# A hybrid decoder layer on one core: one negated copy of the inverse's product bank, one pool of 14 head slots, memory key products in attention's bank, plain scores in four heads

## The chip, the core and the metric

The kernel runs on one core of a Trainium2 chip. A core has five engines with queues of their own: TensorE (PE: matmul, with the weight load, PEld, as a row of its own), VectorE (DVE), ScalarE (ACT), GpSimd (POOL) and SyncE (SP), which here issues the DMA transfers. Results of TensorE land in PSUM, which has eight banks of 128 partitions x 512 fp32; everything else lies in SBUF. The metric is the device time of one execution in microseconds (us), the median of several runs.

## The reference

The trunk has one layer with these inputs: 2048 tokens of width 1024. The token mixer is a gated DeltaNet with 8 heads of width 128 (chunks of 64 in the reference; the kernel uses 128) and, in parallel, cross-attention of 4 heads to 256 memory rows. Both outputs are joined and projected; then come a squared-ReLU MLP of width 4096 and two post-norms. Cut to what the change touches:

```python
lower = where(strict, einsum('bnhcd,bnhsd->bnhcs', k_beta, kc) * decay, 0.0)
a_mat = eye(CHUNK) + lower
u = triangular_solve(a_mat, v_beta, lower=True, unit_diagonal=True)
w = triangular_solve(a_mat, k_beta * exp(gc)[..., None], lower=True, unit_diagonal=True)
attn_qk = einsum('bnhcd,bnhsd->bnhcs', qc, kc) * decay
# scan over chunks, per head:
v_new = u_c - w_c @ state
o = qd @ state + a_c @ v_new
state = state * dc + kd.T @ v_new
# memory:
mem_kv = layer_norm(mem, mem_ln_g, mem_ln_b) @ w_mem_kv
p = softmax(q @ mem_k.T * 128 ** -0.5);  m = p @ mem_v
```

## The kernel before

**Tiles and stages.** The tokens are worked in four blocks of 512 (`TB`), each as four chunks of 128 (`NC`). Two blocks make a half. In a half, `mixer` runs twice (blocks 0 and 1, then 2 and 3), then `out_seven` projects the joined heads of both blocks, `ff1` and `ff2` do the MLP. The three big products are formed by a Strassen-like scheme of seven products. In the profile the first mixer pair fills 0 to about 640 us, the first output projection reaches to 788, the MLP to 1405; the second half follows from there.

**Number formats.** Most products are made of three matmuls on rounded operands (`mm3`): an fp32 value is split into a rounded part hi (a cast on ACT) and a remainder lo (a subtraction on DVE), and hi x hi, hi x lo and lo x hi are added in PSUM. The small products of the DeltaNet are plain fp32 matmuls; each shows as two matmul rows in the trace.

**A head.** `dense` projects q, k and v, applies the convolution and the activation, splits q and k into the tiles kq (hi and lo, one buffer each), and transposes k into kd. `gdn_a` loads the decay rows (gb), builds the decay matrices dl and at, forms the scores pkq of k against k and q, and calls `invert`. `invert` computes the inverse of a unit triangular matrix of 128 per chunk, all four chunks at once: columns of 16 on DVE, and then three joining steps of 16 to 32, 32 to 64 and 64 to 128, each of two products through the banks pq and pp and copies between tiles (Lq, ZP, X32, X64, YP, Y). In the middle step the bank pp is read by a DVE transpose into Lq, and by two multiplications by -1 on DVE and two on ACT into Y. Two further DVE multiplications by -1 place the transposed values into X64. `gdn_b` runs the recurrence chunk by chunk: state, R, vt, state again; at each step TensorE needs the DVE or ACT result before.

**Buffers.** Tiles of 128 x 512 for the heads come from the slot tags s0 and s1, seven each; even heads take s0, odd heads s1 (kd, gb, dl, at, Y, vb, qd). The output projection and the MLP take operand parts from the same tags: xl of the third output product (S3) and of the last (A22) from s1, xl of S4 from s0. PSUM: `acc` has three banks (projections, and the memory keys and values), `ga0` and `ga1` one each (scores, transposes and inverse of even and odd heads), `pb` two (recurrence), `m` one (memory attention).

**Memory.** In block 0, steps 1 to 4 of the head loop also do the memory: `memory_rows` normalizes and transposes it, `memory_keys` loads a weight column, splits it, and forms one head's keys (24 matmuls of 256 columns) in a bank of `acc`, which ACT and DVE then split to a staging tile; two heads per step. `memory_values` does the values. Attention to the memory (`mem_attn`) starts at step 5 of a block.

**Order.** Nothing is issued as written. `Recorder` keeps every operation with its reads and writes; `issue` then plans an order with a price for each operation (`cost`), a delay for each hand-over between engines (`LAT`, `LAT_FROM`, `MARGIN`), free slots of each tag, and a priority, which is the place in the program plus `shift`. The instructions are then emitted in the order of planned starts, and each engine works its queue strictly in that order. A `gate` holds DMA issues back until a given operation. Because all operations are recorded by one helper, the profile gives line 402 for nearly all.

Of the kernel before, what the change touches and what calls it, by code (L numbers as in the profile page):

```python
# [14 lines left out]
P = 128  # L15
# [19 lines left out]
MARGIN = 100  # L35
# [149 lines left out]
class Op:  # L185
    __slots__ = ("i", "eng", "fn", "args", "kw", "dur", "extra", "succ", "npred", "ready", "start", "end", "load", "last",
                 "bufs", "prio", "quads", "cols", "late", "lhs")


class Recorder:  # L190
# [15 lines left out]
    def add(self, eng, fn, name, args, kw):  # L206
        o = Op()
        o.i, o.eng, o.fn, o.args, o.kw = len(self.ops), eng, fn, args, kw
        o.succ, o.npred, o.ready, o.extra = [], 0, 0, 0
# [12 lines left out]
        preds = {}  # L222
# [68 lines left out]
    def issue(self):  # L291
# [50 lines left out]
        while True:  # L342
# [76 lines left out]
def hybrid_layer(  # L419
# [40 lines left out]
    BUFS = {"d": 11, "th": 2, "s0": 7, "s1": 7, "on": 1, "iv": 4}  # L460
# [334 lines left out]
    def dense(b, h, T, G, w0=None):  # L795
        res = {}
        for nm, o in (("q", QO), ("k", KO), ("v", VO)):
# [19 lines left out]
            if nm in "qk":  # L817
# [6 lines left out]
        kd = res["kd"] = slot("kd", "s%d" % (h % 2))  # L824
# [26 lines left out]
    def invert(L, par):  # L851

        Lq = small("Lq", [P, 32, NC], 2)
        for q in range(4):
            r = slice(32 * q, 32 * q + 32)
            nc.scalar.copy(out=Lq[r].rearrange("p f c -> p c f"), in_=L[r, :, 32 * q:32 * q + 32])
# [11 lines left out]
        nc.vector.tensor_scalar_mul(Lc, Lq[:, 0:16], half[:, 0:1])  # L868
        nc.vector.scalar_tensor_tensor(out=Lc, in0=Lq[:, 16:32], scalar=half[:, 1:2], in1=Lc,
# [22 lines left out]
        Y = slot("Y", "s%d" % par)  # L892
# [24 lines left out]
        ZP = Lq.rearrange("p f c -> p (f c)")[:, :64].rearrange("p (c f) -> p c f", c=2)  # L917
# [6 lines left out]
        for p in range(2):  # L924
            for u, eng in ((0, nc.gpsimd), (1, nc.vector)):
                q = quads[2 * p + u]
                eng.tensor_copy(X32[q, :, q].part((u, p)), Z[64 * p:64 * p + 32, 2 * u:2 * u + 2])
        for p in range(2):
            for u, eng in ((0, nc.gpsimd), (1, nc.vector)):
                q = quads[2 * u + p]  # L930
                eng.tensor_copy(X64[q, :, q].part((u, p)), Z[quads[p], 2 * u:2 * u + 2])
# [43 lines left out]
    def gdn_a(h, r, G):  # L975
# [4 lines left out]
        gb = slot("gb", "s%d" % par)  # L980
# [11 lines left out]
        dl = slot("dl", "s%d" % par)  # L992
# [5 lines left out]
        at = slot("at", "s%d" % par)  # L998
# [18 lines left out]
        vb = slot("vb", "s%d" % par)  # L1017
# [3 lines left out]
        qd = slot("qd", "s%d" % par)  # L1021
# [83 lines left out]
    MB = "m"  # L1105
    KEEP_FF = {2: 0, 3: 1, 4: 2}
# [152 lines left out]
    def second_half(ys, T0d, B, between):  # L1259

        homes = {"T3": [slots("d", 4), slots("s0", 4)], "T2": [slots("d", 3), slots("s0", 3), halves("kq0", 1)],
                 "T4": [slots("s1", 3), slots("th", 2), slots("on", 1), halves("kq1", 1)],
                 "T1": [halves("tok", 4)], "B22": [slots("s1", 4), slots("iv", 4)]}
# [30 lines left out]
        for k in K2:  # L1294
            t4[k] = slot("b21", "s1")
# [129 lines left out]
    def ff2(s, x1d):  # L1425
# [35 lines left out]
        def xpart(n, u, last):  # L1461
# [6 lines left out]
            for j in range(2):  # L1468
                hi, lo = slot("xh", "d", F32R), slot("xl", "s%d" % j, F32R)
# [150 lines left out]
    def out_seven(s, x1d, T0d):  # L1620
# [208 lines left out]
```

## Time and profile before

| | us |
|---|---|
| median of three runs | 2762.95 |
| lowest and highest run | 2762.62, 2763.29 |
| the profiled execution, its own time | 2760.71 |
| its span, first to last instruction | 2759.0 |
| TensorE busy in the span | 2719.8 (99%) |
| VectorE busy | 2112.2 (77%) |
| ScalarE busy | 1642.3 (60%) |
| GpSimd busy | 403.7 (15%) |

The profile is of one execution. A row of a group or of a timeline gives engine, operation, output <- inputs, partitions x elements, how often, and after it the idle time of that engine just before and what ended it. A releaser is inferred from semaphores: where the engine named had long been done, it was another. TensorE's granted clock is 1.00 at full speed; the mean over the span is 0.997.

### The profile page before, as it was taken

What the parts mean: (1) busy time and instruction counts of PE and PEld (TensorE: products, weight loads), DVE (VectorE), ACT (ScalarE), POOL (GpSimd) and SP (SyncE); (2) the same over time, 40 slices, a digit from 0 to 9 for tenths busy, and PEclk for the clock granted to TensorE, in tenths of its full rate; (3) what the DMA queues carried; (4) which work ended last, traced back from release to release, by engine and by line L of the source; (5) the groups of instructions that cost most, each with busy time, mean ns of one, the idle gap of its engine ahead of it and who ended that gap; (6) DMA issues with size and microseconds to landing.
All of it is one profiled execution on the core that took longest, in us unless ns stands there. A gap on an engine that the chain in (4) does not pass through costs nothing.

```text
span 2759.0 us, 42405 instructions
## 1 busy us (share of the span) xinstructions
PE 2719.8 (99%) x13589; PEld 2267.0 (82%) x13589; DVE 2112.2 (77%) x5652; ACT 1642.3 (60%) x4082; POOL 403.7 (15%) x1030
## 2 busy tenths in 40 slices
PE   9999999999999999999999999999999999999998
PEld 7888888887788888888888888888887788888887
DVE  7889889998777777665778887888978665657575
ACT  7678767676485556334446676677855655544342
POOL 3233223321000000000023321223201000000000
PEclk9999999999999999999999999999999999999999
DMA  8565558876788888766754344444578744477673
GB/s 327 207 234 205 215 182 288 290 258 228 269 284 302 280 285 297 268 211 205 265 209 149 138 155 174 169 147 159 206 251 280 249 145 152 163 252 243 205 239 116
DMA packets 208543, 613.99 MB, mean 223 GB/s; under 512 B 23072, under 2 KB 32192, under 8 KB 188352
## 3 DMA queue, kind: packets, MB, share of 16 engines
q1 hardware_dynamic: 207888, 611.23, 63.5%
q8 instruction: 107, 1.75, 0.2%
q14 instruction: 116, 0.95, 0.1%
q10 hardware_dynamic: 432, 0.05, 0.0%
HBM read 436.54 MB, written 174.65 MB: 222 GB/s over the span
## 4 chain that ended last, share of the span: by engine, by line
PE 88%; ACT 7%; DVE 4%; issue 1%; POOL 1%; DMA 0%; DVEq 0%; SPq 0%; POOLq 0%; ACTq 0%
PE f2A L402 13%; PE fA L402 12%; PE ao L402 8%; PE f2C L402 6%; PE fC L402 6%; PE az L402 5%; PE aq L402 5%; PE av L402 5%; PE ak L402 5%; PE f2B L402 3%; PE fB L402 3%; PE amq L402 3%; PE pc L402 3%; PE po L402 2%; PE pkq L402 1%
## 5 line engine op out<-in xcount | busy, mean ns | idle before, releaser
L402 DVE TENSOR_TENSOR whl<-wraw,whl 128x512 fp32r<-128x512 f32 (+2 forms) x294 | 257.2, 884 | 109.4 <-ACT whl L402 107.0
L402 ACT CAST whl<-wraw 128x512 fp32r<-128x512 f32 (+2 forms) x294 | 226.5, 780 | 158.0 <-PE fC L402 52.0
L402 PE MATMUL fA<-B,whl 128*128 128x512 f32 x1152 | 277.2, 389 | 1.8 <-ACT B L402 1.5
L402 ACT CAST X<-X 128x1024 fp32r<-128x1024 f32 x118 | 123.9, 1052 | 236.2 <-DMA X<-xsc 196.2
L402 PE MATMUL f2A<-whl,X 128*128 128x512 f32 x1152 | 262.1, 389 | 0.0
L402 PEld LDWEIGHTS fA<-B,whl 128*128 128x128 f32 x1152 | 216.1, 188 | 47.5 <-ACT B L402 1.9
L402 PEld LDWEIGHTS f2A<-whl,X 128*128 128x128 f32 x1152 | 216.2, 188 | 44.9
L402 DVE TENSOR_TENSOR X<-X,X 128x1024 fp32r<-128x1024 f32 x118 | 144.2, 1223 | 129.0 <-ACT X L402 128.8
L402 PE MATMUL aq<-T,whl 128*128 128x512 f32 x768 | 214.3, 408 | 10.0 <-ACT T L402 5.5
L402 PE MATMUL az<-T,whl 128*128 128x512 f32 x768 | 213.0, 406 | 0.0
L402 PE MATMUL ak<-T,whl 128*128 128x512 f32 x768 | 211.4, 406 | 0.0
L402 PE MATMUL av<-T,whl 128*128 128x512 f32 x768 | 210.4, 404 | 0.0
L402 PE MATMUL fC<-B,whl 128*128 128x512 f32 x768 | 185.4, 389 | 0.3 <-DVE B L402 0.3
L402 PE MATMUL f2C<-whl,X 128*128 128x512 f32 x768 | 174.7, 389 | 0.0
L402 PEld LDWEIGHTS fC<-B,whl 128*128 128x128 f32 x768 | 144.1, 188 | 30.7 <-DVE B L402 0.8
L402 PEld LDWEIGHTS f2C<-whl,X 128*128 128x128 f32 x768 | 144.1, 188 | 29.9
L402 PEld LDWEIGHTS aq<-T,whl 128*128 128x128 f32 x768 | 136.5, 191 | 32.7 <-ACT T L402 5.5
L402 POOL TENSOR_SCALAR ve<-mv 128x1 f32<-128x1 f32 x34 | 16.4, 483 | 962.0 <-DVE mv L402 961.5
L402 PEld LDWEIGHTS av<-T,whl 128*128 128x128 f32 x768 | 137.3, 189 | 22.7
L402 PEld LDWEIGHTS ak<-T,whl 128*128 128x128 f32 x768 | 136.4, 189 | 23.5
L402 PEld LDWEIGHTS az<-T,whl 128*128 128x128 f32 x768 | 135.9, 189 | 21.6
L402 PE MATMUL ao<-whl,X 128*128 128x512 f32 x528 | 140.1, 404 | 3.5 <-DVE whl L402 1.3
(287 smaller groups left out, 6300.8 us busy)
## 6 DMA issues: line engine op xcount, KB each, us to landing
whl<-wsc SPq DMA_DIRECT2D x108, 1024.0 KB, 4.8
wraw<-in_w_ff_dram SPq DMA_DIRECT2D x106, 512.0 KB, 4.5
X<-xsc SPq DMA_DIRECT2D x96, 512.0 KB, 3.9
wsc<-whl SPq DMA_DIRECT2D x36, 1024.0 KB, 5.2
whl<-tsc SPq DMA_DIRECT2D x64, 512.0 KB, 4.7
xsc<-hB SPq DMA_DIRECT2D x96, 256.0 KB, 3.4
xo<-cat SPq DMA_DIRECT2D x80, 256.0 KB, 3.9
wraw<-in_w_in_dram SPq DMA_DIRECT2D x35, 512.0 KB, 5.9
```

What stands on the lines that cost most here:

```text
L402: o.fn(*[res(a) for a in o.args], **{k: res(v) for k, v in o.kw.items()})
```

## The change

- **Planner.** Two reads of one PSUM bank from different engines are now ordered in the plan, with a hand-over of 40 ns (`TURN`); before, the plan let them run together.
- **Pool.** The tags s0 and s1 of seven slots become one tag s0 of 14. Every use of s1, in the heads, the output projection and the MLP, takes s0.
- **Memory keys.** The product goes to bank `m` in place of a bank of `acc`, and the load and split of its weights are planned 400 places earlier.
- **Scores.** In heads 5, 6 and 7 of block 1 and head 7 of block 3 (`PLAIN`), q and k are not split, and the scores are two plain fp32 products of 128 columns per chunk in place of three rounded ones of 256.
- **Inverse.** Lq is laid out chunk by chunk, so its four copies write contiguous rows, and Lc reads it with a stride. The four copies into X32 are all on DVE and the four into X64 all on POOL; before, each set was half and half. In the middle step ACT makes one negated copy of bank pp in SBUF (`Nf`, in the second half of Lq), and the transpose, the copies into Y (two DVE, two ACT) and the two into X64 read from it.

```diff
-MARGIN = 100
+MARGIN, TURN = 100, 40
...
+                    elif r.buf.psum and q.eng != eng and not is_w and not qw:
+                        turns[q.i] = q
...
+        for i, q in turns.items():
+            if i not in preds:
+                preds[i] = q
+                q.turns.add(o.i)
...
-                s.ready = max(s.ready, o.end + lat)
+                s.ready = max(s.ready, o.end + (TURN if s.i in o.turns else lat))
...
-    BUFS = {"d": 11, "th": 2, "s0": 7, "s1": 7, "on": 1, "iv": 4}
+    BUFS = {"d": 11, "th": 2, "s0": 14, "on": 1, "iv": 4}
...
     def memory_keys(h):
+        rec.shift = -400
         w = load_cols(w_mem_k, h)
-        a = bank("amk", "acc")
+        rec.shift = 0
+        a = bank("amk", "m")
...
-            if nm in "qk":
+            if nm in "qk" and (b, h) not in PLAIN:
...
-        Lq = small("Lq", [P, 32, NC], 2)
+        Lq = small("Lq", [P, NC, 32], 2)
...
-            nc.scalar.copy(out=Lq[r].rearrange("p f c -> p c f"), in_=L[r, :, 32 * q:32 * q + 32])
+            nc.scalar.copy(out=Lq[r], in_=L[r, :, 32 * q:32 * q + 32])
...
-            for u, eng in ((0, nc.gpsimd), (1, nc.vector)):
+            for u in range(2):
                 q = quads[2 * p + u]
-                eng.tensor_copy(X32[q, :, q].part((u, p)), Z[64 * p:64 * p + 32, 2 * u:2 * u + 2])
+                nc.vector.tensor_copy(X32[q, :, q].part((u, p)), Z[64 * p:64 * p + 32, 2 * u:2 * u + 2])
...
-                eng.tensor_copy(X64[q, :, q].part((u, p)), Z[quads[p], 2 * u:2 * u + 2])
+                nc.gpsimd.tensor_copy(X64[q, :, q].part((u, p)), Z[quads[p], 2 * u:2 * u + 2])
...
-        tr = Lq.rearrange("p f c -> p (f c)")[:64, 64:].part("t")
-        nc.vector.transpose(tr, pb[:64])
+        Nf = Lq.rearrange("p c f -> p (c f)")[:, 64:]
+        nc.scalar.activation(Nf, pb, AF.Copy, scale=-1.0)
+        tr = Lq.rearrange("p c f -> p (c f)")[:64, :64]
+        nc.vector.transpose(tr, Nf[:64])
+        N3 = Nf.rearrange("p (c f) -> p c f", c=2)
         for p in (1, 0):
             o = Y3[64 * p:64 * p + 32, :, 64 * p + 32:64 * p + 64]
-            nc.vector.tensor_scalar_mul(o[:, 2:4], pp[quads[2 * p + 1]], -1.0)
-            nc.scalar.activation(o[:, 0:2], pp[quads[2 * p]], AF.Copy, scale=-1.0)
+            nc.vector.tensor_copy(o[:, 2:4], N3[quads[2 * p + 1]])
+            nc.scalar.copy(out=o[:, 0:2], in_=N3[quads[2 * p]])
...
-            nc.vector.tensor_scalar_mul(X64[quads[2 * u + 1], :, quads[2 * u]].part((u, 2)), tr[quads[u]].part("t"), -1.0)
+            nc.vector.tensor_copy(X64[quads[2 * u + 1], :, quads[2 * u]].part((u, 2)), tr[quads[u]])
...
-        kh, kl = r["kq"]
+        kh, kl = r.get("kq", (None, None))
...
-                mm3(pkq[:, c - c0], kh[:, 0, cs], kl[:, 0, cs], kh[:, :, cs], kl[:, :, cs], True, True)
+                if kh is None:
+                    for u, x in enumerate((k, q)):
+                        nc.tensor.matmul(pkq[:, c - c0, u], k[:, cs], x[:, cs], start=True, stop=True)
+                else:
+                    mm3(pkq[:, c - c0], kh[:, 0, cs], kl[:, 0, cs], kh[:, :, cs], kl[:, :, cs], True, True)
...
+    PLAIN = {(1, 5), (1, 6), (1, 7), (3, 7)}
...
-                lo = slot("xl", "s0" if n == 5 else "s1", F32R)
+                lo = slot("xl", "s0" if n == 5 else "s0", F32R)
```

More of the change, by code (lines that the diff above doesn't have):

```diff
@@ L186 @@
     __slots__ = ("i", "eng", "fn", "args", "kw", "dur", "extra", "succ", "npred", "ready", "start", "end", "load", "last",
-                 "bufs", "prio", "quads", "cols", "late", "lhs")
+                 "bufs", "turns", "prio", "quads", "cols", "late", "lhs")
 class Recorder:
@@ L208, in add @@
         o.i, o.eng, o.fn, o.args, o.kw = len(self.ops), eng, fn, args, kw
-        o.succ, o.npred, o.ready, o.extra = [], 0, 0, 0
+        o.succ, o.npred, o.ready, o.extra, o.turns = [], 0, 0, 0, set()
         o.prio = o.i + self.shift
@@ L221, in add @@
         o.quads = {("r" if v in rd else "w", v.buf.psum): v.p0 // 32 for v in wr + rd[::-1]}
-        preds = {}
+        preds, turns = {}, {}
         for refs, is_w in ((rd, False), (wr, True)):
@@ L823, in dense @@
         ss = small("ss", [P, 2 * NC])
-        kd = res["kd"] = slot("kd", "s%d" % (h % 2))
+        kd = res["kd"] = slot("kd", "s0")
         for n, nm in enumerate("kq"):
@@ L867, in invert @@
         Lc = small("Lc", [P, 16, NC], 2)
-        nc.vector.tensor_scalar_mul(Lc, Lq[:, 0:16], half[:, 0:1])
-        nc.vector.scalar_tensor_tensor(out=Lc, in0=Lq[:, 16:32], scalar=half[:, 1:2], in1=Lc,
+        Lf = Lq.rearrange("p c f -> p f c")
+        nc.vector.tensor_scalar_mul(Lc, Lf[:, 0:16], half[:, 0:1])
+        nc.vector.scalar_tensor_tensor(out=Lc, in0=Lf[:, 16:32], scalar=half[:, 1:2], in1=Lc,
                                        op0=ALU.mult, op1=ALU.add)
@@ L891, in invert @@
         XB, LB, X32, X64, Q = (inv[n] for n in ("XB", "LB", "X32", "X64", "Q"))
-        Y = slot("Y", "s%d" % par)
+        Y = slot("Y", "s0")
         Y3 = v4(Y)
@@ L924, in invert @@
         for p in range(2):
-            for u, eng in ((0, nc.gpsimd), (1, nc.vector)):
+            for u in range(2):
                 q = quads[2 * p + u]
-                eng.tensor_copy(X32[q, :, q].part((u, p)), Z[64 * p:64 * p + 32, 2 * u:2 * u + 2])
+                nc.vector.tensor_copy(X32[q, :, q].part((u, p)), Z[64 * p:64 * p + 32, 2 * u:2 * u + 2])
         for p in range(2):
-            for u, eng in ((0, nc.gpsimd), (1, nc.vector)):
+            for u in range(2):
                 q = quads[2 * u + p]
-                eng.tensor_copy(X64[q, :, q].part((u, p)), Z[quads[p], 2 * u:2 * u + 2])
+                nc.gpsimd.tensor_copy(X64[q, :, q].part((u, p)), Z[quads[p], 2 * u:2 * u + 2])
         for r in quads:
@@ L979, in gdn_a @@
         sc = lambda n, c: G[n][:, h, c:c + 1]
-        gb = slot("gb", "s%d" % par)
+        gb = slot("gb", "s0")
         nc.sync.dma_start(out=gb, in_=G["scr"][4 * h:4 * h + 4].rearrange("c i -> (c i)").partition_broadcast(P))
@@ L991, in gdn_a @@
         bh, vbs = r["bh"], r["vbs"]
-        dl = slot("dl", "s%d" % par)
+        dl = slot("dl", "s0")
         dl3 = v4(dl)
@@ L997, in gdn_a @@
             nc.scalar.activation(dl3[:, c], dl3[:, c], AF.Exp, bias=sc("gc", c), scale=-1.0)
-        at = slot("at", "s%d" % par)
+        at = slot("at", "s0")
         at3 = v4(at)
@@ L1016, in gdn_a @@
         pv = trans(v3, "ptv")
-        vb = slot("vb", "s%d" % par)
+        vb = slot("vb", "s0")
         vb3 = v4(vb)
@@ L1020, in gdn_a @@
             nc.scalar.activation(vb3[:, c], pv[:, c], AF.Copy, scale=vbs[:, c:c + 1])
-        qd = slot("qd", "s%d" % par)
+        qd = slot("qd", "s0")
         nc.scalar.activation(qd, gb, AF.Exp)
@@ L1294, in second_half @@
         for k in K2:
-            t4[k] = slot("b21", "s1")
+            t4[k] = slot("b21", "s0")
             nc.sync.dma_start(out=t4[k], in_=T0d[:, 4 + k])
@@ L1468, in xpart @@
             for j in range(2):
-                hi, lo = slot("xh", "d", F32R), slot("xl", "s%d" % j, F32R)
+                hi, lo = slot("xh", "d", F32R), slot("xl", "s0", F32R)
                 split_in_place(hi, lo, xsc[n][:, 2 * u + j].part(2 * u + j))
```

6 lines of the change are left out of this document (3 added, 3 removed).

## The prediction

> **What bounds the kernel now.** I read the page first: the busy table, the slices, the chain that ended last. The reader is to see that TensorE is the bound nearly everywhere, so that only two things can change the time: the number of matmuls, and the stretches in which TensorE waits or runs at a lower clock.
>
> ```profile
> span 2759.0 us, 42405 instructions
> PE 2719.8 (99%) x13589; PEld 2267.0 (82%) x13589; DVE 2112.2 (77%) x5652; ACT 1642.3 (60%) x4082; POOL 403.7 (15%) x1030
> ...
> PE 88%; ACT 7%; DVE 4%; issue 1%; POOL 1%; DMA 0%; DVEq 0%; SPq 0%; POOLq 0%; ACTq 0%
> ```
>
> Then the busy time by stretch, which shows where the missing time lies (PE busy and its starts, weight loads, DVE, ACT, POOL, granted clock, DMA share, GB/s).
>
> ```profile
> 81.50:91.50 10.00, 5.51 (x24) 4.59 (x23) 9.83 (x45) 2.48 (x5) 0.90 (x2) 0.66 0.22 66
> 604.00:645.00 41.00, 36.74 (x207) 29.55 (x207) 37.59 (x130) 32.16 (x97) 9.13 (x22) 1.00 0.70 237
> 701.00:713.00 12.00, 8.52 (x33) 6.34 (x32) 6.05 (x9) 6.47 (x19) 1.46 (x3) 0.72 0.51 169
> 1096.00:1405.00 309.00, 309.00 (x1368) 254.29 (x1368) 202.32 (x257) 121.11 (x133) 12.40 (x21) 1.00 0.67 229
> ```
>
> The last row is the second MLP product: 309.00 us for 1368 starts, 0.226 us each, nothing idle. The other three are the holes that this change can reach. Outside them and the launch, the edited stages (the two mixers) lose only small waits. The profiled run took 2760.71 us around a span of 2759.0; the median of the runs is 2762.95, so I add the same difference to the median.
>
> **The change part by part.**
>
> *Memory key products in bank m, their weights asked for 400 places earlier.* The hole at 82 us is theirs. Timelines of PE and of DVE there:
>
> ```profile
> 81.52 0.63 PE L402 MATMUL amk<-mT,whl 128*128 128x256 f32 x4
> 86.60 1.19 PE L402 MATMUL aq<-T,whl 128*128 128x512 f32 x2 [4.45 <-DVE Bc L402]
> 87.84 7.06 PE L402 MATMUL amk<-mT,whl 128*128 128x256 f32 x44
> ```
>
> ```profile
> 85.77 0.69 DVE L402 SCALAR_TENSOR_TENSOR cz<-th,az 128x512 f32<-128x512 f32 x1
> ...
> 86.56 1.22 DVE L402 TENSOR_TENSOR whl<-wraw,whl 128x1024 fp32r<-128x1024 f32 x1
> ```
>
> Four key products start, then aq waits 4.45 us. Its bank is one of three in acc, two of them taken by the two key banks; the third was az's, whose last reader (cz on DVE) ends at 86.46, and aq starts at 86.60. The row names Bc because that was DVE's latest work; the bank is my reading. After the idle the clock is 0.66 of full over the window: 44 key matmuls take 7.06 us, 0.16 each, where 256 columns at the rate of the MLP row are about 0.113 to 0.12. The 24 starts of the window are worth 2 x 0.226 + 22 x 0.12 = 3.1 us, so 6.9 of its 10 us are lost. With the keys in m, aq has av's bank, free long before, and the keys' weights come early, so 48 key matmuls (5.8 us) are there to fill. The gain lies between 0 and 6.9. DVE is busy 9.83 of these 10 us, so part of its lateness will show at the next need. I take -5.
>
> *Four heads with plain scores.* Per head the split of k and q goes, and three rounded products of 256 columns per chunk become two fp32 products of 128. Groups by form:
>
> ```profile
> L402 ACT CAST kq<-cq 128x512 fp32r<-128x512 f32 x32 | 20.0, 626 | 5.5 <-DVE cq L402 2.7 <-PE pkq L402 2.6
> ...
> L402 DVE TENSOR_TENSOR kq<-cq,kq 128x512 fp32r<-128x512 f32 x32 | 22.0, 688 | 0.5 <-ACT kq L402 0.2
> ```
>
> The splits of k are of the same form. So ACT loses 2 x 0.63 us and DVE 2 x 0.69 us a head. On TensorE a head now has 12 scores at 0.12, 1.44 us. An fp32 product of 128 columns shows as two rows, and the rate of a row is seen in the first lines of the timeline below: the two of pc start 0.21 us ahead of po, 0.11 each. Eight products are sixteen rows, 1.76 us, so +0.3 a head, bounds 0 and +0.6 (a row at 0.12 and a switch), and +1 for four. The relief is in block 1's heads 5 to 7, where the second hole is, and in block 3's head 7. From 604 to 645 us DVE is busy 37.59 of 41 us and PE idle 4.3; the PE timeline there:
>
> ```profile
> 626.98 0.38 PE L402 MATMUL pc<-vt,kd 128*128 128x128 f32 x2
> 627.19 0.39 PE L402 MATMUL po<-vt,at 128*128 128x128 f32 x2
> ...
> 629.82 0.33 PE L402 MATMUL pmT<-ident,pr 128*128 128x128 f32 x1 [0.33 <-ACT pr L402]
> 631.86 0.66 PE L402 MATMUL pmT<-ident,pr 128*128 128x128 f32 x4 [1.71 <-DVE pm L402]
> ```
>
> The longer wait is for the split of a transposed probability on a full DVE. Heads 5 to 7 free 4.1 us of DVE near here, and the kq tiles, which the output projection's first operand reuses, come free three heads earlier. Bounds 0 and -4.3; I take -1.5, nearer the low end, since attention's own chain is untouched.
>
> *One pool of 14 head slots.* At the end of block 1, head 7 holds all seven odd slots, and the operand parts xl of the third output product are taken from the odd pool alone. Timelines of PE and of SP:
>
> ```profile
> 704.15 0.49 PE L402 MATMUL pc<-vt,kd 128*128 128x128 f32 x2 [0.41 <-ACT vt L402]
> 704.47 0.39 PE L402 MATMUL po<-vt,at 128*128 128x128 f32 x2
> 707.49 2.50 PE L402 MATMUL ao<-whl,xh 128*128 128x512 f32 x5 [2.64 <-ACT whl L402]
> ```
>
> ```profile
> 703.06 1.93 SPq L402 DMA_DIRECT2D xl<-xo  x4
> ```
>
> Four loads are issued only as head 7's last products finish, and PE then has nothing but ao, which waits 2.64 us and goes on at a granted clock of 0.72. The window has 33 starts, worth between 33 x 0.11 = 3.6 and 33 x 0.226 = 7.5 us; with 13 of ao and 20 rows of 128 columns it is 5.1, so 6.9 of its 12 us are lost. With head 6's slots in the same pool the loads can be issued a head earlier. The named releaser is a weight cast (whl), which waits in the same queues; if the weights alone decide, the gain is 0. Bounds 0 and -6.9; I take -4. SP issues no transfer more; the loads only move ahead of the weights' loads, which by that may land later.
>
> *The negated copy, the regrouped copies, the turn of readers in the planner.* In one inverse (timeline, other work left out):
>
> ```profile
> 1560.94 0.53 PE L402 MATMUL pp<-inv 128*128 128x32 f32 x4
> ...
> 1561.57 0.23 DVE L402 STREAM_TRANSPOSE Lq<-pp 64x64 f32<-64x64 f32 x1
> ...
> 1562.48 0.22 ACT L402 ACTIVATE Y<-pp 32x64 f32<-32x64 f32 x1
> 1562.73 0.23 DVE L402 TENSOR_SCALAR Y<-pp 32x64 f32<-32x64 f32 x1 [0.93 <-ACT Y L402]
> 1562.99 0.21 ACT L402 ACTIVATE Y<-pp 32x64 f32<-32x64 f32 x1 [0.29 <-DVE Y L402]
> ...
> 1563.23 0.22 DVE L402 TENSOR_SCALAR Y<-pp 32x64 f32<-32x64 f32 x1 [0.28 <-ACT Y L402]
> ...
> 1564.25 0.41 PE L402 MATMUL pq<-YP,inv 128*128 128x64 f32 x2 [0.63 <-ACT YP L402]
> ```
>
> Five readers of one bank go one after another, DVE and ACT in turn, and PE waits 0.63 us at the end. The Trainium skill, page "PSUM — Partial Sum Buffer", section on bank collisions, says that two engines must not touch one bank in the same 32 partitions at once, reads included, and that the compiler orders them; these alternating rows agree. After the change one ACT copy reads the bank (about 0.22 us, as Y<-pp), and the rest read SBUF with both engines at once. The three turns after the transpose (0.29 + 0.28 + about 0.25) go, one copy and its hand-over (about 0.4) come: some 0.4 us less a head. The price on ACT is 32 x 0.22 = 7 us beside 1642.3 busy, hidden under PE; without that cover it would be 7. The gain is only what PE waits there:
>
> ```profile
> PE pq L402 <- DVE YP L402: 1.4, 5, 0.5
> ...
> PE pq L402 <- ACT YP L402: 1.3, 2, 0.7
> ```
>
> Bounds -2.7 and, if the extra hand-over is late instead, +2.7; I take -1.5. Four X32 copies now on DVE and four X64 on POOL are as many on each engine as before; the contiguous write of Lq and the strided read of it go together, no row shows their difference, and both are hidden: 0, bounds -1 and +1.
>
> *A new order of everything.* The planner's costs change, so every order in the mixers is new, with small waits where it guesses wrong. The existing ones are the size to go by: +1, bounds -2 and +5.
>
> Sum: -5 +1 -1.5 -4 -1.5 +1 = **-10 us**: a span near 2749, runs near **2753**.
>
> *The clock.* The clock drop of the 704 us hole followed an idle of 2.64 us, that of the 82 us hole one of 4.45, while the 1.71 us wait at 631 left 1.00 over its window. So a new wait of over 2.6 us costs about twice its length, and one under 1.7 its length alone. The Trainium skill, "TensorE: Matmul & The Clock Gate", section "What's actually happening", puts the drop after an idle window of about 3.4 us; by that the 2.64 us wait would have kept its clock, and the third hole would be worth about 4 instead of 6.9. The row has 0.72, and the measurement decides.
>
> **The rivals.**
> (1) *DVE is the true bound of the early stretch and the hole moves.* For it: 9.83 of 10 us busy. Against: the stretch behind 100 us holds PE full with the same DVE work per head. The -5 goes to 0 and the slot pool gives half: -10 +5 +2 = -3, some 2760, within 0.2%.
> (2) *Slower: bank m is one bank, so the second key product of a pair waits for the first to be drained.* The drain is an ACT cast and a DVE subtraction, and DVE was 4 to 5 us late at 82 us. If both pairs stall like the old hole (6.9 each, clock drop included) and the old hole stays too: +13.8 +5 -10 = +9, so 2772. It decides from a stall of about 2.6 us in each pair, since there the clock drops as well. Against it: the weights come 400 places earlier, and q's 24 products (5.4 us) can stand between the two.
> (3) *All holes close:* -6.9 -6.9 -4.3 -2.7 +1 = -20, so 2743.
> (4) *The change does not do what it says:* the third hole waits for the weights, and the relief of DVE is not on any path; with the first hole closed -5 +1 +1 = -3, as (1).
>
> **How the numbers follow.** A measurement of this kernel tells 0.2%, 5.5 us, from no change: faster means under 2757.4, slower over 2768.5. Forecast (2746 to 2757) 0.50; all holes close 0.16; rivals 1 and 4 together 0.20, mostly within 0.2%; slower 0.14. Faster: 0.50 + 0.16 + 0.02 of the third; same 0.18; slower 0.14. The range goes from the closed holes with their bounds, 2740, up to 2768, the upper end of rivals 1 and 4; the likeliest case's own is 2746 to 2757.
>
> **What would show it.** Right: no idle of 4 us near 82 us and one clock drop fewer before 100 us; amk followed by aq without a wait; xl loads issued several us before head 7's last product and no drop at 705 us; one reader of the first product bank pp, and pq waiting for YP under 1 us in all; 16 rows of pkq in four heads. Wrong: a wait of PE for mst between key products, a hole of over 2.6 us elsewhere in a mixer, or the wait for whl at 704 us unchanged.

## The result and the profile after

The changed kernel takes **2735.2 us** (2734.8 to 2736.7) against 2763.1 us for the kernel before on the same chip: 27.9 us less, a ratio of 0.9903 (95% interval 0.9891 to 0.9915). The forecast was 2753, a gain of 10, and the range ended at 2740. The sign was right; the gain was almost three times the forecast.

The page of the kernel after (span; busy time, share and count of each engine; the chain that ended last):

```profile
span 2733.3 us, 42460 instructions
PE 2710.0 (99%) x13605; PEld 2267.3 (83%) x13605; DVE 2109.6 (77%) x5644; ACT 1636.4 (60%) x4106; POOL 403.2 (15%) x1030
...
PE 92%; DVE 4%; ACT 2%; issue 1%; DMA 1%; POOL 1%; SPq 0%; DVEq 0%; POOLq 0%; ACTq 0%
```

TensorE still bounds the kernel. It has 16 more rows than before (the plain scores) and yet ends 25.7 us sooner, so the whole gain is time in which it stood idle, started its matmuls further apart than it can, or ran at a lower clock. The stretches in which the prediction looked for the holes, and the second MLP product (columns as in the prediction: length, then busy time and starts of PE, PEld, DVE, ACT and POOL, granted clock, DMA share, GB/s):

```profile
81.50:91.50 10.00, 10.00 (x62) 8.74 (x61) 10.00 (x41) 5.81 (x11) 1.55 (x3) 1.00 0.51 177
590.00:645.00 55.00, 53.97 (x315) 45.91 (x314) 51.19 (x190) 41.00 (x130) 14.85 (x38) 1.00 0.62 228
693.00:705.00 12.00, 11.43 (x51) 8.60 (x50) 7.07 (x10) 6.56 (x19) 1.46 (x3) 1.00 0.60 190
1081.40:1390.88 309.48, 309.48 (x1371) 254.83 (x1370) 202.86 (x258) 121.48 (x133) 12.94 (x22) 1.00 0.68 229
```

All three holes are gone: 10.00 of 10 us busy where it was 5.51, 11.43 of 12 where it was 8.52, and no clock under 1.00 in any row. The MLP product has not changed. Closed holes are worth at most 6.9 + 6.9 + 4.3 us by the prediction's own count, though, and its three terms for them came to -10.5. To find the rest I took, for each stage, the time between two landmarks of the PE timeline less the work between them. The work is the number of starts times the median distance from one start to the next in the trace of before (0.227 us for 512 columns, 0.119 for 256, 0.110 for 128 or fewer). What is left is TensorE's **loss**: every wait, named or not, starts that come late while the row still counts PE as busy, and the clock.

| loss of TensorE, us | before | after | difference |
|---|---|---|---|
| block 0 with the memory | 17.7 | 15.0 | -2.7 |
| mixer of block 1 | 13.9 | 8.3 | -5.6 |
| first output projection | 13.2 | 5.8 | -7.4 |
| first MLP | 0.3 | 0.3 | 0 |
| mixers of blocks 2 and 3 | 16.2 | 8.9 | -7.2 |
| second output projection and its MLP | 7.2 | 3.0 | -4.1 |
| matmul work over all | 2676.2 | 2677.6 | +1.3 |

The differences add up to -25.7, the difference of the two profiled executions (2760.71 and 2735.04 us). Almost half of it, 11.3 us, lies in stages in which the prediction saw next to nothing to win: blocks 2 and 3, where PE shows 584.73 us busy of 588.26 (row below), and the second output projection with its MLP. Of the 16.2 us that before loses in blocks 2 and 3 only 3.5 are idle in PE's row at a clock of 1.00; the rest is starts that come late.

### The profile page after: what moved, and what is told of

Its sections match the earlier page's. It is cut to its first block, busy times and chain, and to the rows that moved or that the text cites. A ratio compares the mean times of both kernels' runs of the same rounds, so it can differ in the third digit from the quotient of the medians.

```text
span 2733.3 us, 42460 instructions
## 1 busy us (share of the span) xinstructions
PE 2710.0 (99%) x13605; PEld 2267.3 (83%) x13605; DVE 2109.6 (77%) x5644; ACT 1636.4 (60%) x4106; POOL 403.2 (15%) x1030
## 4 chain that ended last, share of the span: by engine, by line
PE 92%; DVE 4%; ACT 2%; issue 1%; DMA 1%; POOL 1%; SPq 0%; DVEq 0%; POOLq 0%; ACTq 0%
PE f2A L408 13%; PE fA L408 12%; PE ao L408 8%; PE f2C L408 6%; PE aq L408 6%; PE av L408 6%; PE fC L408 6%; PE az L408 6%; PE ak L408 6%; PE f2B L408 3%; PE pc L408 3%; PE amq L408 3%; PE fB L408 3%; PE po L408 2%; PE pkq L408 2%; PE pq L408 1%
## 5 line engine op out<-in xcount | busy, mean ns | idle before, releaser
L408 PE MATMUL aq<-T,whl 128*128 128x512 f32 x768 | 219.9, 411 | 5.6 <-ACT T L408 5.6
```

The costliest lines, as they stand in the source:

```text
L408: o.fn(*[res(a) for a in o.args], **{k: res(v) for k, v in o.kw.items()})
```

## The experiments

Each kernel below was timed against the kernel before on the same chip. The question was whether the gain is (P) each edit closing the hole at its own place, (L) a lucky order, since any edit makes the planner redraw the whole order, or (I) the new inverse relieving every mixer; the expectations use these letters.

### The order alone, first pair: MARGIN 110

```diff
-MARGIN = 100
+MARGIN = 110
```

The kernel before, and the kernel after, with no other edit: the same instructions in another planned order.

> The kernel before with the planner's margin for a hand-over at 110 ns in place of 100: no instruction is added or left out, only the order is planned anew. It measures what a new order alone is worth. Theory P (each edit closes the hole at its own place): within 4 us of before, and the 7 us holes near 82 and 704 us still there in some form. Theory L (any new order moves the waits about, and the gain of the changed kernel is a better draw): a difference of 6 us or more either way, with holes at other places.

> The changed kernel with the planner's margin at 110 ns in place of 100: the same instructions in a newly planned order. The first four runs (the kernel before with another margin: +14 us; with one edit alone: +4 to +5 each) speak for theory L, that the order decides as much as the edits. Theory L: the changed kernel loses 6 to 18 us of its 26 by this alone (2741 to 2753), with holes of over 1.5 us and clock drops at new places. Theory P (the edits close holes for good): within 4 us of 2735.

Measured: before's goes to 2775.7 (ratio 1.0050, 1.0037 to 1.0062), after's to 2754.9 (0.9972, 0.9962 to 0.9982). An order is worth 13 to 20 us by itself. The prediction's term for this was +1, with bounds of -2 and +5.

### One part taken out of the kernel after

Without the planner's turn of readers:

```diff
-MARGIN, TURN = 100, 40
+MARGIN = 100
...
-                    elif r.buf.psum and q.eng != eng and not is_w and not qw:
-                        turns[q.i] = q
```

> The changed kernel without the planner's turns; no instruction changes. Theory L: another draw, 2739 to 2752. Theory P, the plan must know the turns: +3 to +6 in the mixers, at the inverse. Theory N (turns no longer matter since one ACT copy reads the bank): within 2 us.

Without the move of the memory keys:

```diff
-        rec.shift = -400
         w = load_cols(w_mem_k, h)
-        rec.shift = 0
-        a = bank("amk", "m")
+        a = bank("amk", "acc")
```

> The changed kernel with the memory keys back in a bank of acc and without the early load. Theory P: the hole at 82 us with its clock drop is back, +3 to +7 before 330 us and nothing later. Theory L: the early hole is back and the rest is drawn anew, so 2738 to 2755 with changes of over 3 us in stages that the edit does not touch.

Without the common pool (all slots of odd heads and xl back in s1):

```diff
-    BUFS = {"d": 11, "th": 2, "s0": 14, "on": 1, "iv": 4}
+    BUFS = {"d": 11, "th": 2, "s0": 7, "s1": 7, "on": 1, "iv": 4}
...
-        gb = slot("gb", "s0")
+        gb = slot("gb", "s%d" % par)
```

> The changed kernel with two pools of seven. Theory P: xl waits again for head 7, a hole of over 2 us and a clock drop at the end of block 1, +5 to +10, in the first output projection above all. Theory L: that hole and further changes of over 3 us elsewhere, 2738 to 2755.

Without the new inverse (all of it: layout of Lq, copies to X32 and X64, negated copy):

```diff
-        Nf = Lq.rearrange("p c f -> p (c f)")[:, 64:]
-        nc.scalar.activation(Nf, pb, AF.Copy, scale=-1.0)
-        nc.vector.transpose(tr, Nf[:64])
+        nc.vector.transpose(tr, pb[:64])
...
-            nc.vector.tensor_copy(o[:, 2:4], N3[quads[2 * p + 1]])
+            nc.vector.tensor_scalar_mul(o[:, 2:4], pp[quads[2 * p + 1]], -1.0)
```

> The changed kernel with the inverse as before (five readers of the product bank, copies split half and half, Lq transposed). In all five kernels with the new inverse so far, whatever their order, blocks 2 and 3 lose 9 to 12 us to waits, in the five with the old one 13 to 19. Theory I (the shorter inverse is what the mixers gain by): +5 to +9 over blocks 1 to 3, in every block some, TensorE's waits for YP back. Theory L (a better draw): the mixers stay within 3 us of the changed kernel, changes are elsewhere.

Without the plain scores (q and k split and multiplied in three products in all heads):

```diff
-            if nm in "qk" and (b, h) not in PLAIN:
+            if nm in "qk":
```

> The changed kernel with split scores in all heads. Theory P: work on TensorE is 1.3 us less, but DVE and ACT have 4 splits more at the ends of blocks 1 and 3, so +2 to +6 in the output projections. The rival that the plain scores matter little: -2 to +2 by TensorE's work alone. Theory L: another draw, up to 15 us more in the output projections, as with the other margin.

Measured: without the turn 2740.1 (0.9916, 0.9902 to 0.9929), keys 2741.7 (0.9927, 0.9914 to 0.9939), plain scores 2747.8 (0.9950, 0.9938 to 0.9963), pool 2753.8 (0.9968, 0.9955 to 0.9980), inverse 2755.7 (0.9975, 0.9966 to 0.9984). They are 5, 7, 13, 19 and 20 us slower than the kernel after, 63 together for a gain of 28. So they don't add up, and the part of each can't be read from its own run.

For the keys the trace does show the place. The same stretch with the keys back in acc and with the change (windows of the kernel without the move, then of the kernel after):

```profile
80.00:94.00 14.00, 9.29 (x44) 8.14 (x43) 12.16 (x50) 5.50 (x13) 2.04 (x3) 0.76 0.27 74
```

```profile
80.00:94.00 14.00, 14.00 (x86) 12.29 (x85) 14.00 (x56) 7.92 (x16) 1.55 (x3) 1.00 0.50 147
```

And the PE timelines (start, length, product, count, idle before it), without the move and after:

```profile
82.56 0.63 PE L408 MATMUL amk<-mT,whl 128*128 128x256 f32 x4
86.68 0.77 PE L408 MATMUL aq<-T,whl 128*128 128x512 f32 x2 [3.49 <-DVE Bc L408]
88.68 7.50 PE L408 MATMUL amk<-mT,whl 128*128 128x256 f32 x41 [1.23 <-DVE whl L408]
```

```profile
82.15 3.04 PE L408 MATMUL amk<-mT,whl 128*128 128x256 f32 x24
85.02 5.31 PE L408 MATMUL aq<-T,whl 128*128 128x512 f32 x22
90.17 3.04 PE L408 MATMUL amk<-mT,whl 128*128 128x256 f32 x24
93.04 0.63 PE L408 MATMUL aq<-T,whl 128*128 128x512 f32 x2
```

With the move, 24 key products, 22 of q and 24 key products follow without a gap; the second product of the pair doesn't wait for the bank, and q's products stand between, as the prediction had it against rival 2. With the other edits in place, the hole of 3.49 us and the clock of 0.76 come back when the keys are in acc and their weights are not asked for early; the two halves of this edit were not tried apart. In the traces of all kernels here but the one with the pool under before's order, aq waits 3.5 to 4.5 us, until some point between 86 and 88 us, in eight of the nine with the keys in acc (not in before at MARGIN 90) and in none of the ten with the move. One of these ten, after at MARGIN 90, has a wait of 3.34 us of av at 90 us instead.

### One part put into the kernel before

The edits are the lines above the other way round.

> The kernel before with the memory keys alone in bank m and their weights planned 400 places earlier. Theory P: the hole at 82 us closes, with its clock drop; as the changed kernel's trace loses 4 us more than before between 100 and 160 us, the net is -2 to -7 us, all of it before 330 us, and nothing later beyond 3 us. Theory L: a difference unlike that at places the edit does not touch (blocks 1 to 3).

> The kernel before with one pool of 14 slots alone. Theory P: the loads of xl are issued some us before the last products of head 7, no clock drop near 704 us, and -4 to -8 us in the first output projection; the second half's projection gains 2 to 4. The rival that the weights decided there: the wait of PE for whl stays, and the gain is under 2 us. Theory L: unlike both, with the difference spread over the mixers.

> The kernel before with the planner told of the turns of two readers of one bank; no instruction changes. Theory P: the plan fits the chip better in the inverse, so TensorE's waits for YP go and the small waits in the mixers shrink: -2 to -6 us over the four blocks. If the turns matter only with the single negated copy: within 2 us. Theory L: 6 us or more either way.

> The kernel before with the new inverse alone. Theory I: -5 to -9 us in blocks 1 to 3 (waits there as in the changed kernel, near 8 and 9 us), the early hole at 82 us unchanged, the output projections within 3 us unless the draw is bad. Theory L: the mixers as before, 13 to 16 us each pair.

Measured: keys 2765.6 (1.0014, 1.0005 to 1.0023), pool 2764.8 (1.0009, 1.0001 to 1.0018), turn 2765.9 (1.0018, 1.0009 to 1.0027), inverse 2762.4 (1.0001, 0.9993 to 1.0010). No part alone gains anything in total. The pool alone does what was forecast for it in the first output projection, which loses 6.5 us instead of 13.2, with no clock drop near 704 us, but the second one then loses 13.6 instead of 7.2. Still, the inverse alone does in the mixers what it does in the kernel after. Blocks 2 and 3, from the first aq of block 2 to the first ao, as windows of: the kernel before; before with the keys; before with the inverse; after without the plain scores; before with the turn.

```profile
1405.54:1993.80 588.26, 584.73 (x3286) 496.02 (x3285) 488.42 (x1917) 405.56 (x1385) 158.17 (x445) 1.00 0.47 169
```

```profile
1408.12:1996.29 588.17, 584.62 (x3287) 495.97 (x3285) 488.58 (x1917) 405.02 (x1385) 158.07 (x445) 1.00 0.47 169
```

```profile
1403.51:1985.09 581.58, 580.92 (x3283) 495.87 (x3281) 484.20 (x1913) 398.93 (x1395) 158.94 (x445) 1.00 0.48 171
```

```profile
1397.04:1978.33 581.29, 581.01 (x3286) 496.10 (x3285) 489.40 (x1919) 404.62 (x1400) 158.60 (x445) 1.00 0.48 170
```

```profile
1410.60:1995.40 584.80, 583.62 (x3283) 496.02 (x3281) 489.19 (x1915) 402.77 (x1383) 158.04 (x445) 1.00 0.48 170
```

The first, second and fourth row hold as many matmuls (3285 weight loads each) in 588.26, 588.17 and 581.29 us, the third four fewer in 581.58: 7 us less with the new inverse, alone or with the other edits. The turn alone, which changes no instruction, takes 3.5 us off these blocks (last row, also with four matmuls fewer). In the kernel with the inverse alone the 7 us are then given back in the output projections, which lose 30.9 us instead of 20.4.

### The pool alone, in before's own order

All slots of s0 and s1 are taken from one pool of 14 when the instructions are issued, while the order is planned with seven and seven, so that the order stays that of before.

```diff
+            if self.pool.name == "sp" and tag in ("s0", "s1"):
+                tag, bufs = "s0", 14
```

> The kernel before with one pool of 14 in the program that is issued, while the planner still plans with two of seven: every engine's order of instructions is that of before, only the buffers differ. It takes the new order out of the pool's effect. Theory P (the two pools made xl wait for head 7): the wait near 704 us shrinks by 2 to 5 us and its clock drop goes, and nothing else moves by over 1 us: -3 to -7. If the order decides (the loads stand late in SP's queue, or the weights come late): within 1 us of before everywhere.

Measured: 2760.1, ratio 0.9995 (0.9986 to 1.0004), no difference. SP's and PE's timelines at the third hole:

```profile
699.52 3.83 SPq L405 DMA_DIRECT2D xl<-xo  x4
```

```profile
706.99 2.50 PE L405 MATMUL ao<-whl,xh 128*128 128x512 f32 x5 [2.63 <-ACT whl L405]
```

The four xl loads are issued at 699.52 instead of 703.06 us, as the prediction wanted it, and ao waits 2.63 us for whl instead of 2.64. So the weights decide that hole, as rival 4 said, and not the slots that head 7 holds. The clock drop at this hole lasts 3.4 us here and 6.8 in before, and a drop of 3.4 us at 631 us is new; the last section comes back to it. The keys in bank m under before's own order were not tried.

### Six more orders: MARGIN 90, 95 and 105

The same constant at three more values, in before and in after, to tell the edits from the order. With MARGIN 100 and 110 that makes five orders of either kernel.

> Kernel before with the planner's MARGIN at 90 instead of 100: the same instructions in another planned order. Theory P (the edits, by what they do in any order, are the gain): near 2763, as the orders of before seen so far (2762 to 2776), blocks 2 and 3 lose 13 to 19 us beside the matmul work. Theory L (a lucky order is the gain): some order of before should come under 2755 too, with output projections that lose under 12 us. Expected 2769, between 2760 and 2778.

> Kernel after with MARGIN 90: all edits, another planned order. Theory P: within 5 us of 2735. Theory L: like MARGIN 110, which gave 2755: 2745 to 2760, the output projections again lose 19 us or more, while the mixers of blocks 2 and 3 stay at 8 to 12 us lost in either theory. Expected 2751.

> Kernel before with MARGIN 105: as with 90. Theory P 2763; theory L anything from 2750 to 2776, without relation to the size of the step in MARGIN. Expected 2769, between 2760 and 2778.

> Kernel after with MARGIN 105: as with 90. Theory P within 5 us of 2735; theory L 2745 to 2760. Between both families of orders (before at 90, 100, 105, 110; after at the same) the difference of the means is the part of the gain that the edits give in any order; expected -16, between -11 and -22.

> Kernel before with MARGIN 95, a fifth planned order of the same instructions. The four orders so far gave 2763.1, 2767.7, 2769.7 and 2775.7, mean 2769. Expected 2768, between 2760 and 2778; if the edits are the gain, no order of before comes under the mean of after's orders, 2747.

> Kernel after with MARGIN 95. The four orders so far gave 2735.2, 2742.7, 2754.9 and 2756.7, mean 2747. Expected 2747, between 2735 and 2758. If the order of MARGIN 100 is a lucky one, this is slower than 2735 by 5 us or more; either way blocks 2 and 3 should lose 8 to 12 us in the mixers.

| MARGIN | before: us, ratio (interval) | after: us, ratio (interval) | difference, us |
|---|---|---|---|
| 90 | 2767.7, 1.0019 (1.0010 to 1.0027) | 2742.7, 0.9929 (0.9916 to 0.9943) | -25.0 |
| 95 | 2777.2, 1.0052 (1.0038 to 1.0065) | 2758.0, 0.9985 (0.9976 to 0.9994) | -19.2 |
| 100 | 2763.1, 1 | 2735.2, 0.9903 (0.9891 to 0.9915) | -27.9 |
| 105 | 2769.7, 1.0031 (1.0019 to 1.0042) | 2756.7, 0.9981 (0.9972 to 0.9989) | -13.0 |
| 110 | 2775.7, 1.0050 (1.0037 to 1.0062) | 2754.9, 0.9972 (0.9962 to 0.9982) | -20.8 |

The mean difference is -21.2 us (about -14 to -28 from the spread of the five differences, -9 to -34 if the two kernels' orders are taken as unrelated). The slowest order of after beats the fastest of before, so the five edits together gain in any of these orders; that each does it at its own place, as theory P has it, does not follow. Both kernels have their fastest order at MARGIN 100: before's lies 7.6 us under the mean of its five, after's 14.3. The difference of these, 7 us of the 28, is the order (L).

### Which part gives what

The loss by stage in all kernels (block 0; mixers of blocks 1, 2 and 3 together; both output projections, the second with the MLP behind it). The first MLP is left out: it loses 0.3 us in before and after, and up to 5 in other orders. "b +x" is before with x, "a -x" is after without x.

| kernel | block 0 | mixers 1-3 | outputs |
|---|---|---|---|
| before, MARGIN 100 | 17.7 | 30.0 | 20.4 |
| before, 90 / 95 | 14.8 / 22.5 | 26.6 / 32.1 | 28.9 / 26.1 |
| before, 105 / 110 | 22.9 / 20.0 | 29.5 / 29.3 | 28.2 / 29.3 |
| b +keys | 16.5 | 28.9 | 24.6 |
| b +pool | 20.3 | 31.0 | 20.1 |
| b +turn | 20.0 | 21.3 | 31.7 |
| b +inverse | 15.6 | 17.2 | 30.9 |
| a -inverse | 18.5 | 23.7 | 20.5 |
| after, MARGIN 100 | 15.0 | 17.2 | 8.9 |
| after, 90 / 95 | 16.0 / 19.7 | 16.5 / 18.1 | 13.9 / 25.0 |
| after, 105 / 110 | 17.9 / 16.2 | 19.9 / 18.2 | 22.2 / 22.5 |
| a -turn | 17.8 | 19.3 | 8.9 |
| a -keys | 23.0 | 17.2 | 8.9 |
| a -pool | 13.2 | 15.3 | 31.2 |
| a -plain scores | 14.5 | 18.1 | 21.4 |

A least-squares fit over these 19 kernels, one term per edit, gives (with the standard error): in block 0 the keys -4.5 (1.6); in the mixers the inverse -8.8 (1.4) and the turn -4.5 (1.4); in the outputs the pool -11.1 (3.5). In the mixers the two edits don't add up, so these are means: they lose 26.6 to 32.1 us with neither, 21.3 and 23.7 with the turn alone, 17.2 and 19.3 with the inverse alone, 15.3 to 19.9 with both. The inverse is worth some 11 us without the turn and some 5 beside it, and the turn next to nothing beside the new inverse. The fit of the measured times gives the inverse -9.7, the pool -7.7, the plain scores -5.3, the keys -1.3 and the turn +0.8, each with an error of about 5 to 6: there only the inverse reaches twice its error, and even that is not clear of zero. The remaining scatter of one order is 7.4 us. The fit takes the 19 as separate draws, and they are not quite: from block 2 on, after without the keys has PE's order of after, row for row.

The mixers are the clearest. The ten kernels with the new inverse lose 15.3 to 19.9 us there, the nine with the old one 21.3 to 32.1. **What in the inverse does it** shows in part. Groups by form (busy time and mean ns; idle before, and what ended it), of before and of after:

```profile
L402 ACT COPY Lq<-dl 32x128 f32<-32x128 f32 x128 | 53.4, 417 | 4.1 <-DVE dl L402 2.9
...
L402 DVE TENSOR_SCALAR Y<-pp 32x64 f32<-32x64 f32 x64 | 14.2, 222 | 7.7 <-ACT Y L402 6.1
L402 ACT ACTIVATE Y<-pp 32x64 f32<-32x64 f32 x64 | 13.7, 214 | 18.4 <-PE pp L402 10.3 <-DVE Lq L402 4.9 <-DVE Y L402 1.9
...
L402 DVE SCALAR_TENSOR_TENSOR Lc<-Lq,half,Lc 128x64 f32<-128x64 f32 x32 | 9.0, 282 | 0.2
...
L402 DVE TENSOR_SCALAR Lc<-Lq,half 128x64 f32<-128x64 f32 x32 | 8.0, 250 | 4.5 <-ACT Lq L402 4.1
```

```profile
L408 ACT COPY Lq<-dl 32x128 f32<-32x128 f32 x128 | 37.6, 294 | 6.1 <-DVE dl L408 4.7
...
L408 ACT COPY Y<-Lq 32x64 f32<-32x64 f32 x64 | 15.5, 243 | 1.7
...
L408 DVE COPY Y<-Lq 32x64 f32<-32x64 f32 x64 | 11.9, 186 | 2.0
L408 DVE SCALAR_TENSOR_TENSOR Lc<-Lq,half,Lc 128x64 f32<-128x64 f32 x32 | 11.8, 367 | 0.5
L408 DVE TENSOR_SCALAR Lc<-Lq,half 128x64 f32<-128x64 f32 x32 | 9.6, 302 | 2.9 <-ACT Lq L408 2.7
...
L408 ACT ACTIVATE Lq<-pp 128x64 f32<-128x64 f32 x32 | 7.2, 224 | 8.1 <-PE pp L408 8.0
```

ACT and DVE stood blocked 18.4 + 7.7 us ahead of the copies into Y, with everything queued behind them; now it is 1.7 + 2.0, with 8.1 ahead of the new copy. Of the 18.4, though, 10.3 ended with the product pp itself, as 8.0 of the 8.1 do now; what the turns cost is at most some 8 us on each of the two engines. And the contiguous write makes the four Lq copies 123 ns shorter each: 15.8 us less on ACT, half a microsecond at the head of each inverse, against 4.4 us more on DVE, whose strided reads into Lc went from 250 and 282 to 302 and 367 ns. The step itself got no shorter. One inverse after the change (timeline, other work left out):

```profile
1539.87 0.53 PE L408 MATMUL pp<-inv 128*128 128x32 f32 x4
...
1541.09 0.24 ACT L408 ACTIVATE Lq<-pp 128x64 f32<-128x64 f32 x1
1541.37 0.24 DVE L408 STREAM_TRANSPOSE Lq<-Lq 64x64 f32<-64x64 f32 x1 [0.29 <-ACT Lq L408]
1541.63 0.40 DVE L408 COPY Y<-Lq 32x64 f32<-32x64 f32 x2
1541.94 0.51 ACT L408 COPY Y<-Lq 32x64 f32<-32x64 f32 x2
...
1543.78 0.55 PE L408 MATMUL pq<-YP,inv 128*128 128x64 f32 x4
```

The copies now run on both engines at once (1541.63 and 1541.94), but from the first pp to pq<-YP the median of 32 heads is 3.22 us, against 2.94 before; with the turn alone it is 3.22 too. PE simply has other work planned for that time: its loss ahead of pq in blocks 1 to 3 is 5.7 us smaller than before (mean of five orders each), and 3.1 and 4.5 smaller in the two kernels where the old inverse is planned with the turn. I read this as the plan knowing when the copies end, once their turns are priced or gone; it would be about half of the mixers' gain. With the turn alone ACT and DVE still stand blocked 15.2 + 3.4 us ahead of the copies into Y, and the mixers lose 21.3 us instead of 30.0, which speaks for the plan and not for the blocked engines. Which of the two halves of the edit, the layout or the negated copy, gives the rest was not separated.

**The outputs.** Waits of PE in the first output projection (who waits for what: us in total, times, longest), in the kernel after, and after without the pool:

```profile
PE ao L408 <- ACT xh L408: 0.6, 1, 0.6
PE ao L408 <- DVE whl L408: 0.5, 1, 0.5
```

```profile
PE ao L408 <- DVE whl L408: 3.6, 3, 2.4
```

The kernels without the pool in their plan lose 20.4 to 31.7 us in the outputs, those with it 8.9 to 25.0; the longest waits are those of ao for whl, the split weights. So the pool works through the order that it lets the planner draw, not through the slots at head 7's end. The groups overlap, and three kernels with the pool lose 8.9 each (two of them with one order in the second half) while the others lose 13.9 to 25.0, so this part is less certain than the inverse's.

**The plain scores.** Their price is as forecast: the work went from 2676.2 to 2677.6 us. These groups are the 32 products of the four heads, two rows each, which take the place of 48 products at 256 columns:

```profile
L408 PE MATMUL pkq<-kq 128*128 128x256 f32 x336 | 57.0, 293 | 0.3 <-DVE at L408 0.3
...
L408 PE MATMUL pkq<-cq,ck 128*128 128x128 f32 x32 | 6.3, 278 | 0.0
L408 PE MATMUL pkq<-ck 128*128 128x128 f32 x32 | 6.2, 274 | 0.0
```

Without them the kernel after takes 2747.8, less than the mean of after's five orders (2749.5). A gain of theirs is not shown.

No run beat the kernel after; the next is the one without the turn, 2740.1.

## Why the prediction was wrong

The direction and the list of edits that matter were right, the sizes were not. Step by step:

- **Memory keys, -5 (bounds 0 and -6.9): right at its place.** The hole at 82 us closed with its clock drop; in block 0 the fit gives -4.5 (1.6). From 75 to 100 us the loss fell from 7.0 to 0.2, but from 100 to 160 us it rose from 1.6 to 5.7, and with the keys alone by as much. So block 0 gained only 2.7 between before and after, and 1.2 with the keys alone: much of what rival 1 held.
- **Plain scores, +1 and -1.5: the price right** (+1.3), the gain not shown.
- **One pool, -4: the mechanism failed.** "The loads can be issued a head earlier" came true in before's order and closed nothing; the named releaser, the weight cast, had been the true one, as rival 4 held. The pool's gain comes through the plan, in both output projections: -11.1 (3.5) there and -7.7 (4.9) in the times. The bound of -6.9 covered one hole in one of them.
- **The inverse, -1.5 (bounds -2.7 and +2.7): the step that failed most.** I bounded it by PE's named waits of pq for YP. These did fall from 2.7 to 0.5:

```profile
PE pq L408 <- ACT YP L408: 0.5, 1, 0.5
```

  But the term, which covered the new inverse and the turn of readers, is worth about 12 us in the mixers: they lose 29.6 us in the mean with neither and 17.7 with the new inverse. Nor did the step get "some 0.4 us less a head": from pp to pq<-YP it takes 3.22 us instead of 2.94. Most of what TensorE loses in the mixers are waits too short or too mixed to be put down to one releaser. The loss of the mixers, 30 us in blocks 1 to 3, was to be had from the trace of before by counting starts, and it was the true upper bound. I also put the new layout of Lq, with the regrouped copies, at 0 between -1 and +1; it took 15.8 us of busy time off ACT, at the head of every inverse, though what that is worth alone was not measured. The Trainium skill, page "SBUF — State Buffer", section "Door 1: The DMA port swizzle", says in a note that SBUF has lines of 16 bytes, four fp32, and that each access that crosses to a new line pays a penalty. The old copies wrote with a stride of just 16 bytes, a new line for each element, and 417 against 294 ns agrees. The prediction did not use it. Its reading of the alternating rows of Y<-pp was too quick as well: it took them to agree with the rule that it cites there, for the same 32 partitions, but by the code each of these four copies reads 32 partitions of its own, and they took turns all the same. What ordered them is not shown.
- **A new order, +1 (bounds -2 and +5): mis-sized.** Ten orders of two kernels scatter by 14 us in the one and 23 in the other. In this draw it gave -7.
- **The clock.** "One under 1.7 its length alone" was wrong, as the last section shows. The drop at the third hole did not follow its wait of 2.64 us either: it began at 705.70 us, inside it (704.85 to 707.49).

In the prediction's form the sum comes to: inverse and turn -9 to -12, pool -8 to -11, keys -1 to -5, plain scores not shown, together -21 (the mean of five orders each), and the order -7. Rival 3 (2743) had the nearest time, though its reasons were only the holes. Rival 2 did not happen.

## What to carry to other kernels

Where a bound engine works a planned queue, take a stage's possible gain from its length less the work of its starts, not from the waits that the profile can name. An edit that makes the planner redraw everything is measured together with one draw of the order: shift a constant that has no meaning for the work, run both kernels in several orders, and compare the families. And the reads of one bank that two engines take in turn seem to have cost most here in what the plan didn't know of them: told of the turns, with no instruction changed, the mixers lost 21.3 us instead of 30.0.

## What the runs showed of the hardware that was not expected

**The clock falls after a poorly filled stretch, without a long idle.** All drops ahead of the tail, in all traces, last 3.4, 6.8 or 10.2 us, steps of 3.4. In the kernel after without the turn, PE had its longest idle near 124 us with 1.12 us (timeline), and windows of 3.4 us before and after that point show:

```profile
124.47 0.78 PE L402 MATMUL pc<-R,Y 128*128 128x128 f32 x2 [1.12 <-DVE R L402]
```

```profile
121.10:124.50 3.40, 2.21 (x13) 1.32 (x11) 1.39 (x7) 2.72 (x12) 0.33 (x1) 1.00 1.01 417
124.50:127.90 3.40, 3.40 (x16) 3.30 (x17) 1.01 (x5) 2.84 (x12) 0.00 (x0) 0.50 0.98 411
```

With PE busy 2.21 of 3.40 us, the next 3.40 us ran at 0.50. Where a wait falls matters too. Before, and before with the pool in its own order, have the same order of PE's instructions and the same wait of 1.71 us near 631 us. In before (first two rows) a step of 3.41 us ends within the wait, and no drop follows; in the other (last two) the wait lies within one step, PE is busy 1.38 of 3.41 us, and the next step runs at 0.50:

```profile
627.20:630.61 3.41, 2.63 (x14) 1.62 (x12) 2.96 (x17) 3.41 (x17) 0.41 (x2) 1.00 0.87 306
630.61:634.03 3.42, 2.17 (x14) 1.78 (x15) 2.70 (x12) 3.42 (x11) 1.06 (x2) 1.00 0.56 223
```

```profile
628.07:631.48 3.41, 1.38 (x9) 0.86 (x8) 2.64 (x15) 3.41 (x14) 1.50 (x3) 1.00 0.90 342
631.48:634.90 3.42, 3.06 (x14) 2.69 (x14) 2.99 (x10) 3.41 (x9) 0.00 (x0) 0.50 0.35 68
```

Other waits of up to 1.84 us were followed by no drop. In each trace the clock's changes lie whole steps of 3.41 us apart. I counted such steps at full clock in all twenty traces by what their matmul starts are worth (0.227, 0.119 and 0.110 us as above): with under 30% of the step all 34 were followed by half rate, from 30 to 40% 13 of 17, from 40 to 60% 6 of 83, the one at 121.10 among them, and above that none. The Trainium skill, "TensorE: Matmul & The Clock Gate", section "What's actually happening", has a free-running window of about 3.4 us and a drop after an idle window. The length of the drops and the fixed steps agree; that the window must be idle does not. What decides in the steps between 30 and 60% is not shown.

**A strided write on ACT costs 123 ns in 417** for 32 partitions of 128 fp32 (294 contiguous; 416 or 417 and 294 in all twenty traces, whatever the order), while the same layout read with a stride costs DVE 52 and 85 ns for 128 partitions of 64.
